# Pool projection of a decoder trunk, token-major: four seven-product units spread over three column groups, block moves split over two queues

## The chip, the cores and the metric

The kernel runs on one core of a Trainium2 chip. The metric is the device time of one execution in microseconds (us); for the kernel before it is 2051.21 us, the median of three runs (2050.52 to 2051.46). The core has five engines, each with its own instruction queue that runs in order: TensorE (PE), VectorE (DVE), ScalarE (ACT), GpSimd (POOL) and SyncE (SP). SP, POOL and ACT issue the transfers here.

## The reference

A decoder trunk of two layers on 256 tokens of 2048 channels, all in float32. Layer 0 mixes by causal pooling in four channel groups, layer 1 by dilated attention; each is followed by a gated convolutional feed-forward part, and each sublayer by a residual sum and a layer norm. What the change touches is the pooling mixer and the norm after it:

```python
def pool_mixer(h, w_in, w_grp, scale, w_out):
    p = (h @ w_in).reshape(B_, S, N_POOL_GROUPS, POOL_GROUP_DIM).astype(jnp.float32)
    ...
        outs.append((c - lag) / cnt - p[:, :, g])          # trailing mean over window 2, 4, 8, 16, less the token
    pooled = jnp.stack(outs, axis=2).astype(h.dtype)
    mixed = jnp.einsum('bsgc,gcd->bsgd', pooled, w_grp).reshape(B_, S, D) * scale
    return mixed @ w_out
...
        h = layer_norm(DEEPNORM_ALPHA * h + mix, ln1_g[i], ln1_b[i])
        ff = conv_ffn(h, ffn_w_up[i], ffn_conv_w[i], ffn_conv_b[i], ffn_w_down[i])
```

## The kernel before

**Precision and units.** Every float32 factor is split into a high part in a format that PE multiplies fast (float32r) and a low part with the rest; a product is three matmuls (high by high, high by low, low by high). The weights come in blocks of 512 x 512, one block a *unit*. For each unit SP loads the block (`raw`, L89), ACT copies the high part (`wh`, L99) and DVE subtracts it for the low part (`wl`, L100). `run_units` walks a list of units: at unit i it queues the load of unit i + 5 and the split of unit i + 3, then the matmuls of unit i, then whatever earlier steps put off to this point by `later(n, step)`, then the unit's own `post`. So the order of instructions in each engine's queue is fixed by the order of units and by these counts. Three `raw` blocks and four pairs of split weights can live at a time. PSUM holds four tiles of two banks each (`pair`, `two_banks`).

**Sevens.** A 2 x 2 blocked product normally takes eight block products. A unit given to `mk_seven` takes seven, by sums of blocks on both sides. It is two units in the list: "a" with 18 matmuls of 256 columns (three products) and "b" with 24 (four products). Its weights are prepared by `split_sums`: for "a" a copy on ACT (L119) and four subtractions on DVE (L120 to L124); for "b" two copies (L113) and two subtractions (L114). The sums on the activations' side come from `summed`, which makes `msums[g]` for a pool group g. Sevens use an extra pair of PSUM banks ("s"); when the last seven of a group is done, `early_post` folds those banks into a scratch tile, which POOL adds to the residual by an accumulating transfer (`onto`, L290) after the group's end, or DVE adds directly.

**The pool layer's end.** `pool_post` does the pooling, `grp_post` scales the group product, either through `summed` or by four scaled pairs (L628 on ACT, L629 on DVE). The output projection has tokens on the partitions (token-major, `group_tm`): four column groups c0 to c3 of 512 channels, each summing over four row blocks j, in the order written out in the last loop of the block. Before, c0 is all plain and comes among the last pool units; c1 and c2 have blocks 1 and 0 as sevens, c3 has 1 and 0 as sevens with block 2 last. The posts add the result to the residual `HT[c]` (L689, L691).

**Back to features.** The next part wants channels on the partitions. `begin` takes statistics of c0, finds a first mean and shifts all four groups by it (L711). `landed(c)` takes the statistics of a group and calls `to_features`: DVE transposes 32 x 32 blocks (L559), and `moves` sends 16 block transfers (L546) that put the blocks in place; for c0 to c2 by SP in three portions over three units, for c3 all at once over SP, POOL and ACT. Then `xp(c)` makes the scaled copy `XP[c]` (L427 on ACT, L428 on DVE) on which the feed-forward's first gate product runs before the norm is known. `ended` closes the statistics with c3, and `chain_tm` spreads them over the partitions: four copies on ACT (L450), then eight matmuls (`spread`, L455), put off by one unit, so that PE has the first gate unit ahead of it. `normed` and `norm_evac` then apply the norm.

The order of the units around the change, before: c0 block 3, c0 block 2, product of group 0, c0 block 1, c1 block 3, c0 block 0, and from there on c1 to c3 in their order; then the feed-forward's four gate units, the first ones that read `XP`.

Of the kernel before, what the change touches and what calls it, by code (L numbers as in the profile page):

```python
# [9 lines left out]
F32 = mybir.dt.float32  # L10
# [7 lines left out]
T = 256  # L18
# [14 lines left out]
def trunk(ctx: ExitStack, tc: tile.TileContext, x, pool_w_in, pool_w_grp, pool_scale, pool_w_out,  # L33
# [501 lines left out]

    def moves(fr, to, at_once=False):
        fr = fr.rearrange("p (k b j) -> p b k j", k=8, b=4)
        dst = []

        def part(i, n):  # L540
            if i == 0:
                dst.append(to().rearrange("p (k a j) -> p a k j", k=8, a=4))
            for ab in range(i, i + n):
                a, b = ab // 4, ab % 4
                by = (nc.sync, nc.gpsimd, nc.sync, nc.gpsimd, nc.scalar)[ab % 5] if at_once else nc.sync
                by.dma_start(dst[0][32 * b:32 * b + 32, a], fr[32 * a:32 * a + 32, b])  # L546

        if at_once:
            part(0, 16)
            return  # L550
        for k, (i, n) in enumerate(((0, 6), (6, 5), (11, 5))):
            later(k + 1, lambda i=i, n=n: part(i, n))

    def to_features(c, at_once=False):
        hb = hp.tile([P, 4, T], F32, name="hb", tag="h")
        hf = hb.rearrange("p m t -> p (m t)")
        V.transpose(hf.rearrange("p (m t c) -> p t m c", m=4, t=2), HT[c].rearrange("p t (m c) -> p t m c", m=4))  # L559

        def to():
            H[c] = hp.tile([P, 4, T], F32, name="h", tag="h")
            return H[c].rearrange("p m t -> p (m t)")

        moves(hf, to, at_once)

# [54 lines left out]
    def grp_post(g):  # L621
        def post(ps):
            mixed_q[g] = t = quad_tile("mixed")
            if g < 2:
                return summed(g, ps)
            for m in range(4):
                sc = vec[0][:, 64 + 4 * g + m:65 + 4 * g + m]
                A.activation(t[:, m, 0, :T], ps[m][:, :T], AF.Copy, scale=sc)  # L628
                V.scalar_tensor_tensor(t[:, m, 1, :T], ps[m][:, :T], sc, t[:, m, 0, :T].bitcast(F32),  # L629
                                       op0=OP.mult, op1=OP.subtract)  # L630
        return post
# [3 lines left out]
    def summed(g, ps):  # L635
# [8 lines left out]
        def two():  # L644
# [3 lines left out]
            V.tensor_tensor(d[3], a12, d[1], OP.subtract)  # L648
            hl = [pools["pool"].tile([P, 4, PADW + T], F32R, name="ms", tag=("pb", "sw")[g], bufs=2)[:, :, :T]
                  for i in range(2)]  # L650
            A.copy(hl[0], f)
# [33 lines left out]
    def out_post(c):  # L685
        def post(t, ps, half=None):
# [5 lines left out]
            if c == 3:  # L692
                ended(t)
            elif t == 1:
                if c == 0:
                    later(1, begin)
                later(2, lambda: landed(c))
                later(6, lambda: xp(c, 0, 0))
        return post

    def begin():
        ST["bn"] = bn = lnp.tile([P, 2, 5, 6], F32, name="bn", tag="bn")
        for t in range(2):
            mv = lnp.tile([P, 6], F32, name="mv", tag="mv", bufs=2)
            V.bn_stats(bn[:, t, 0, :], HT[0][:, t, :])
            V.bn_aggr(mv[:, 0:2], bn[:, t, 0:1])
            V.tensor_scalar(mv[:, 2:3], mv[:, 0:1], -1.0, None, op0=OP.mult)
            V.tensor_scalar(bn[:, t, 0, 1::3], bn[:, t, 0, 1::3], mv[:, 0:1], None, op0=OP.subtract)
            for c in range(4):
                y = HT[c][:, t, :]  # L710
                A.activation(y, y, AF.Identity, scale=1.0 if c == 0 else ALPHA, bias=mv[:, 2:3])  # L711

    def landed(c):
        if c > 0:
            for t in range(2):
                V.bn_stats(ST["bn"][:, t, c, :], HT[c][:, t, :])
        to_features(c)

    ends = []

    def ended(t):
# [5 lines left out]
        if t == 1:  # L727
            to_features(3, True)
        V.reciprocal(mv[:, 3:4], mv[:, 2:3])
# [6 lines left out]
    mark = len(units)  # L736
    for c, js in enumerate(((3, 2, 1, 0), (3, 1, 2, 0), (3, 1, 2, 0), (3, 1, 0, 2))):
        sv = {i: (lambda j=j: msums[j]) for i, j in enumerate(js) if c > 0 and j < 2}
        group_tm(pool_w_out[0], [(512 * j, 512) for j in js], 512 * c, 512, [lambda j=j: mixed_q[j] for j in js],
                 out_post(c), seven=sv, early=early_post(c, c < 3))  # L740
    outs = units[mark:]
    del units[mark:]
    units.extend(outs[:2])
    add_grp(0)
    units.extend([outs[2], outs[4], outs[3]] + outs[5:])
    marks.append(len(units))
# [540 lines left out]
    with tc.tile_pool(name="pool", bufs=1) as pp:  # L1287
        pools["pool"] = pp
        pools["pb"] = [pp.tile([P, 4, PADW + T], F32, name=f"pb{i}", tag="pb", bufs=2) for i in range(2)]
        for b in pools["pb"]:  # L1290
            V.memset(b[:, :, :PADW], 0.0)
        vrow, crow = [], []
        for l in range(2):
            n = 80 if l == 0 else 64
# [5 lines left out]
            vrow.append((r, n))  # L1300
            cr = pp.tile([2 * NF, 4, P], F32, name=f"crow{l}")
            nc.gpsimd.dma_start(cr[:, 0:3, :], ffn_conv_w[l].rearrange("j (k p) -> k j p", p=P))
# [87 lines left out]
```

## Time and profile before

| | |
|---|---|
| time, median of 3 runs | 2051.21 us |
| profiled execution | 2050.99 us, span 2049.2 us |
| PE busy | 2012.0 us (98%) |
| DVE busy | 1759.0 us (86%) |
| ACT busy | 1283.3 us (63%) |
| POOL busy | 100.2 us (5%) |
| granted TensorE clock, mean | 0.993 |
| weights and inputs read | 380.01 MB, 186 GB/s over the span |

The span is the time from the first to the last instruction. PE is busy in nearly all of it; matmuls are pipelined and their ends are modelled, so a busy PE need not be at its peak. The granted clock is the share of its full speed that PE was allowed. In a table of waits the idle time of an engine is put down to what came last; a chain of waits runs back from the last instruction. "x3" behind a line is a count, and a name such as `wl` stands for all buffers of that name.

### The profile page before, as it was taken

The numbers are of one execution on the slowest core, as the hardware profiler recorded it, in microseconds if no ns is written. First come the engines' busy times: TensorE is split into PE (matmuls) and PEld (weight loads), VectorE is DVE, ScalarE is ACT, GpSimd is POOL, SyncE is SP. The second block draws the span as 40 slices with busy tenths as digits, with TensorE's granted clock in tenths as the row PEclk, the third lists the DMA queues.
The fourth block names the chain that finished last, engine by engine and source line by source line (L and its number), as shares of the span: only waits on it lengthen the run. The fifth ranks groups of instructions, "written<-read, shape, count | busy, mean of one in ns | idle before, by whom it ended". The sixth has DMA issues, their size and how long they took to land.

```text
span 2049.2 us, 31450 instructions
## 1 busy us (share of the span) xinstructions
PE 2012.0 (98%) x12679; PEld 1811.1 (88%) x12679; DVE 1759.0 (86%) x1856; ACT 1283.3 (63%) x1567; POOL 100.2 (5%) x163
## 2 busy tenths in 40 slices
PE   9998599999999999999999999999999999999999
PEld 8887598899989989889898988998899989999987
DVE  6878787899899989879897868887799899989898
ACT  5454487766677667655654434568767676667673
POOL 2000100000000000000010111000000000000000
PEclk9999899999999999999999999999999999999999
DMA  8555667666756666886466666547666657676665
GB/s 246 205 174 148 178 208 206 165 221 199 226 177 216 208 227 183 237 249 201 165 166 220 202 182 198 189 161 223 190 198 219 216 168 227 198 230 197 202 213 181
DMA packets 287841, 410.91 MB, mean 201 GB/s; under 512 B 90366, under 2 KB 101524, under 8 KB 287440
## 3 DMA queue, kind: packets, MB, share of 16 engines
q1 hardware_dynamic: 274448, 390.74, 58.8%
q0 software_dynamic: 12000, 17.42, 5.6%
q8 instruction: 99, 1.62, 0.3%
q10 hardware_dynamic: 1248, 0.75, 0.1%
q14 instruction: 46, 0.38, 0.1%
HBM read 380.01 MB, written 2.10 MB: 186 GB/s over the span
## 4 chain that ended last, share of the span: by engine, by line
PE 88%; DVE 6%; DMA 3%; ACT 2%; issue 1%; SPq 1%; ACTq 0%; DVEq 0%
PE acc L180 39%; PE acc L181 20%; PE s L249 3%; PE s L247 3%; PE s L248 3%; PE t L249 2%; PE t L248 2%; PE t L247 2%; PE t L258 2%; PE t L259 2%; PE t L260 2%; PE acc L184 2%; PE acc L185 2%; PE acc L183 2%; DVE wl L100 2%
## 5 line engine op out<-in xcount | busy, mean ns | idle before, releaser
L180 PE MATMUL acc<-xc,wh 128*128 128x512 f32 x3264 | 1151.6, 396 | 0.0
L181 PE MATMUL acc<-xc,wl 128*128 128x256 f32 x3264 | 915.9, 281 | 0.9 <-DVE wl L100 0.9
L100 DVE TENSOR_TENSOR wl<-raw,wh 128x2048 fp32r<-128x2048 f32 (+2 forms) x298 | 641.6, 2160 | 162.2 <-ACT wh L99 157.6
L180 PEld LDWEIGHTS acc<-xc,wh 128*128 128x128 f32 x3264 | 616.0, 189 | 142.8 <-issue 0.3
L99 ACT CAST wh<-raw 128x2048 fp32r<-128x2048 f32 (+2 forms) x298 | 535.9, 1804 | 156.7 <-PE acc L180 53.9
L181 PEld LDWEIGHTS acc<-xc,wl 128*128 128x128 f32 x3264 | 615.2, 188 | 1.3 <-DVE wl L100 1.2
L113 ACT CAST wh<-raw 128x1024 fp32r<-128x1024 f32 x156 | 162.9, 1053 | 219.5 <-DVE raw L122 195.6
L114 DVE TENSOR_TENSOR wl<-raw,wh 128x1024 fp32r<-128x1024 f32 x156 | 186.1, 1222 | 16.0 <-ACT wh L113 16.0
L121 DVE TENSOR_TENSOR wl<-raw,wh 128x1536 fp32r<-128x1536 f32 x78 | 136.8, 1754 | 7.0 <-ACT wh L119 5.7
L119 ACT CAST wh<-raw 128x1536 fp32r<-128x1536 f32 x78 | 115.3, 1478 | 41.1 <-PE acc L180 24.5
L290 POOL DMA_DIRECT2D ht<-w x52 | 44.8, 1009 | 1440.0 <-DVE ht L977 582.7
L249 PE MATMUL t<-wh,g 128*128 128x256 f32 x376 | 105.6, 281 | 0.0
L248 PE MATMUL t<-wl,g 128*128 128x256 f32 x376 | 105.5, 280 | 0.0
L247 PE MATMUL t<-wh,g 128*128 128x256 f32 x376 | 105.5, 280 | 0.0
L785 ACT ACTIVATE c<-u,cv 128x256 f32<-128x256 f32 x172 | 89.5, 593 | 24.1 <-DVE f L847 16.4
L124 DVE TENSOR_TENSOR raw<-raw 128x1024 f32<-128x1024 f32 x78 | 95.6, 1225 | 2.7
L249 PE MATMUL s<-wh,xs 128*128 128x256 f32 x344 | 96.0, 279 | 0.0
L247 PE MATMUL s<-wh,xs 128*128 128x256 f32 x344 | 96.0, 279 | 0.0
L248 PE MATMUL s<-wl,xs 128*128 128x256 f32 x344 | 95.9, 279 | 0.0
L790 ACT ACTIVATE a<-u,cv 128x256 f32<-128x256 f32 x172 | 73.5, 500 | 11.9 <-DVE g L857 11.9
L776 ACT COPY u<-acc 128x512 f32<-128x512 f32 x84 | 46.7, 573 | 42.9 <-PE acc L181 42.8
L790 ACT ACTIVATE u<-u,cv 128x256 f32<-128x256 f32 x172 | 73.5, 501 | 0.0
(386 smaller groups left out, 3450.8 us busy)
## 6 DMA issues: line engine op xcount, KB each, us to landing
raw<-in_ffn_w_up_dram SPq DMA_DIRECT2D x160, 1024.0 KB, 5.1
raw<-in_ffn_w_down_dram SPq DMA_DIRECT2D x80, 1024.0 KB, 5.4
raw<-in_pool_w_out_dram SPq DMA_DIRECT2D x16, 1024.0 KB, 5.5
raw<-in_shared_w_k_dram SPq DMA_DIRECT2D x16, 1024.0 KB, 5.2
raw<-in_attn_w_q_dram SPq DMA_DIRECT2D x16, 1024.0 KB, 5.0
raw<-in_shared_w_v_dram SPq DMA_DIRECT2D x16, 1024.0 KB, 5.3
raw<-in_attn_w_o_dram SPq DMA_DIRECT2D x16, 1024.0 KB, 5.2
ht<-w POOLq DMA_DIRECT2D x54, 256.0 KB, 5.2
```

The lines of the kernel that those rows point to most:

```text
L99: A.copy(wh[i][:, s], r[:, s])
L100: V.tensor_tensor(wl[i][:, s], r[:, s], wh[i][:, s].bitcast(F32), OP.subtract)
L113: A.copy(h[:, :, n], r[:, :, n])
L114: V.tensor_tensor(l[:, :, n], r[:, :, n], h[:, :, n].bitcast(F32), OP.subtract)
L119: A.copy(hs, rs)
L121: V.tensor_tensor(ls, rs, hs.bitcast(F32), OP.subtract)
L180: PE.matmul(ps[m].ap, h[:, k, c], q[:, k, :, :T], start=st, stop=False)
L181: PE.matmul(ps[m][:, :T], l[:, k, c], q[:, k, 0, :T], start=False, stop=sp)
L247: PE.matmul(to, xh, h[:, k, n], start=opens and kk == 0, stop=False)
L248: PE.matmul(to, xh, l[:, k, n], start=False, stop=False)
L249: PE.matmul(to, xl, h[:, k, n], start=False, stop=ends and kk == 1)
L790: A.activation(to[:, m, :], u[:, m, i:i + T], AF.Copy, scale=cv[:, i, j:j + 1])
```

## The change

1. *Sevens.* All four column groups take the blocks in the order 3, 2, 1, 0. c0 has blocks 2 and 1 as sevens, c1 and c2 block 1, c3 none: four in place of six. Pool groups 1 and 2 make sums now, group 0 goes by the scaled pairs. c0's sums too are added by POOL.
2. *Order of units.* c0 block 3, both halves of c0's block 2, product of group 0, both halves of c0's block 1, c1 block 3, c0 block 0, and then the rest in order.
3. *Block moves.* For c0 to c2 POOL issues moves 0 to 7 and SP moves 8 to 11 at once, and SP the last four one unit later. For c3 the sixteen are dealt out anew: six to SP, seven to POOL, three to ACT.
4. *Scaled copies and shift.* `begin` comes two units after c0's end in place of one, c0's `landed` three in place of two, and `xp` 7, 5 and 5 units after the group's end in place of 6. The shift of c0 and c1 stays in `begin`, that of c2 and c3 comes two and three units later.
5. *Buffers.* The sums of group 2 lie in a block buffer of the `h` kind and in one that the convolution's parameter rows used earlier.

```diff
@@ -533,7 +533,7 @@
         return hp.tile([P, 4, T], F32, name="ht", tag="h").rearrange("p a t -> p (a t)").rearrange(
             "p (t c) -> p t c", t=2)
 
-    def moves(fr, to, at_once=False):
+    def moves(fr, to, by=None):
         fr = fr.rearrange("p (k b j) -> p b k j", k=8, b=4)
         dst = []
 
@@ -542,18 +542,18 @@
                 dst.append(to().rearrange("p (k a j) -> p a k j", k=8, a=4))
             for ab in range(i, i + n):
                 a, b = ab // 4, ab % 4
-                by = (nc.sync, nc.gpsimd, nc.sync, nc.gpsimd, nc.scalar)[ab % 5] if at_once else nc.sync
-                by.dma_start(dst[0][32 * b:32 * b + 32, a], fr[32 * a:32 * a + 32, b])
-
-        if at_once:
-            part(0, 16)
+                (by[ab] if by else nc.sync).dma_start(dst[0][32 * b:32 * b + 32, a], fr[32 * a:32 * a + 32, b])
+
+        if by:
+            part(0, 12)
+            later(0 if by[12] is nc.gpsimd else 1, lambda: part(12, 4))
             return
         for k, (i, n) in enumerate(((0, 6), (6, 5), (11, 5))):
             later(k + 1, lambda i=i, n=n: part(i, n))
 
 
 
-    def to_features(c, at_once=False):
+    def to_features(c, by=None):
         hb = hp.tile([P, 4, T], F32, name="hb", tag="h")
         hf = hb.rearrange("p m t -> p (m t)")
         V.transpose(hf.rearrange("p (m t c) -> p t m c", m=4, t=2), HT[c].rearrange("p t (m c) -> p t m c", m=4))
@@ -562,7 +562,7 @@
             H[c] = hp.tile([P, 4, T], F32, name="h", tag="h")
             return H[c].rearrange("p m t -> p (m t)")
 
-        moves(hf, to, at_once)
+        moves(hf, to, by)
 
 
     def early_post(c, by_dma):
@@ -621,7 +621,7 @@
     def grp_post(g):
         def post(ps):
             mixed_q[g] = t = quad_tile("mixed")
-            if g < 2:
+            if g in (1, 2):
                 return summed(g, ps)
             for m in range(4):
                 sc = vec[0][:, 64 + 4 * g + m:65 + 4 * g + m]
@@ -646,8 +646,10 @@
             V.tensor_tensor(d[1], d[0], a11, OP.subtract)
             V.tensor_tensor(d[2], a21, a11, OP.subtract)
             V.tensor_tensor(d[3], a12, d[1], OP.subtract)
-            hl = [pools["pool"].tile([P, 4, PADW + T], F32R, name="ms", tag=("pb", "sw")[g], bufs=2)[:, :, :T]
-                  for i in range(2)]
+            if g == 1:
+                hl = [pools["pool"].tile([P, 4, PADW + T], F32R, name="ms", tag="sw", bufs=2)[:, :, :T] for i in range(2)]
+            else:
+                hl = [hp.tile([P, 4, T], F32R, name="ms", tag="h"), pools["pool"].tile([P, 4, T], F32R, name="ms", tag="ms")]
             A.copy(hl[0], f)
             V.tensor_tensor(hl[1], f, hl[0].bitcast(F32), OP.subtract)
             msums[g] = [[z[:, i].rearrange("p (k t) -> p k t", k=2) for z in hl] for i in range(4)]
@@ -693,28 +695,35 @@
                 ended(t)
             elif t == 1:
                 if c == 0:
-                    later(1, begin)
-                later(2, lambda: landed(c))
-                later(6, lambda: xp(c, 0, 0))
+                    later(2, begin)
+                later(3 if c == 0 else 2, lambda: landed(c))
+                later((7, 5, 5)[c], lambda: xp(c, 0, 0))
         return post
 
     def begin():
         ST["bn"] = bn = lnp.tile([P, 2, 5, 6], F32, name="bn", tag="bn")
+        mvs = []
         for t in range(2):
             mv = lnp.tile([P, 6], F32, name="mv", tag="mv", bufs=2)
             V.bn_stats(bn[:, t, 0, :], HT[0][:, t, :])
             V.bn_aggr(mv[:, 0:2], bn[:, t, 0:1])
             V.tensor_scalar(mv[:, 2:3], mv[:, 0:1], -1.0, None, op0=OP.mult)
             V.tensor_scalar(bn[:, t, 0, 1::3], bn[:, t, 0, 1::3], mv[:, 0:1], None, op0=OP.subtract)
-            for c in range(4):
+            mvs.append(mv)
+
+        def less(c):
+            for t in range(2):
                 y = HT[c][:, t, :]
-                A.activation(y, y, AF.Identity, scale=1.0 if c == 0 else ALPHA, bias=mv[:, 2:3])
+                A.activation(y, y, AF.Identity, scale=1.0 if c == 0 else ALPHA, bias=mvs[t][:, 2:3])
+
+        for c in range(4):
+            later((0, 0, 2, 3)[c], lambda c=c: less(c))
 
     def landed(c):
         if c > 0:
             for t in range(2):
                 V.bn_stats(ST["bn"][:, t, c, :], HT[c][:, t, :])
-        to_features(c)
+        to_features(c, 8 * [nc.gpsimd] + 8 * [nc.sync])
 
     ends = []
 
@@ -725,7 +734,7 @@
         V.bn_aggr(mv[:, 0:2], bn[:, t, :4])
         A.activation(mv[:, 2:3], mv[:, 1:2], AF.Sqrt, bias=epst)
         if t == 1:
-            to_features(3, True)
+            to_features(3, (3 * [nc.sync, nc.gpsimd, nc.scalar, nc.gpsimd] + [nc.gpsimd, nc.sync, nc.sync, nc.sync]))
         V.reciprocal(mv[:, 3:4], mv[:, 2:3])
         V.tensor_tensor(mv[:, 4:5], mv[:, 0:1], mv[:, 3:4], OP.mult)
         ends.append(mv)
@@ -734,15 +743,15 @@
             later(2, lambda: xp(3, 0, 0))
 
     mark = len(units)
-    for c, js in enumerate(((3, 2, 1, 0), (3, 1, 2, 0), (3, 1, 2, 0), (3, 1, 0, 2))):
-        sv = {i: (lambda j=j: msums[j]) for i, j in enumerate(js) if c > 0 and j < 2}
+    for c, js in enumerate(((3, 2, 1, 0), (3, 2, 1, 0), (3, 2, 1, 0), (3, 2, 1, 0))):
+        sv = {i: (lambda j=j: msums[j]) for i, j in enumerate(js) if j in ((1, 2), (1,), (1,), ())[c]}
         group_tm(pool_w_out[0], [(512 * j, 512) for j in js], 512 * c, 512, [lambda j=j: mixed_q[j] for j in js],
-                 out_post(c), seven=sv, early=early_post(c, c < 3))
+                 out_post(c), seven=sv, early=early_post(c, True))
     outs = units[mark:]
     del units[mark:]
-    units.extend(outs[:2])
+    units.extend(outs[:3])
     add_grp(0)
-    units.extend([outs[2], outs[4], outs[3]] + outs[5:])
+    units.extend(outs[3:5] + [outs[6], outs[5]] + outs[7:])
     marks.append(len(units))
 
 
@@ -1286,10 +1295,11 @@
         run_units(3)
     with tc.tile_pool(name="pool", bufs=1) as pp:
         pools["pool"] = pp
-        pools["pb"] = [pp.tile([P, 4, PADW + T], F32, name=f"pb{i}", tag="pb", bufs=2) for i in range(2)]
+        pools["pb"] = [pp.tile([P, 4, PADW + T], F32, name=f"pb{i}") for i in range(2)]
         for b in pools["pb"]:
             V.memset(b[:, :, :PADW], 0.0)
         vrow, crow = [], []
+        crows = pp.tile([P, 2, 4, P], F32, name="crow", tag="ms")
         for l in range(2):
             n = 80 if l == 0 else 64
             r = pp.tile([80, P], F32, name=f"vrow{l}")
@@ -1298,7 +1308,7 @@
             if l == 0:
                 nc.gpsimd.dma_start(r[64:80], pool_scale[0].rearrange("(k p) -> k p", p=P))
             vrow.append((r, n))
-            cr = pp.tile([2 * NF, 4, P], F32, name=f"crow{l}")
+            cr = crows[:2 * NF, l]
             nc.gpsimd.dma_start(cr[:, 0:3, :], ffn_conv_w[l].rearrange("j (k p) -> k j p", p=P))
             nc.gpsimd.dma_start(cr[:, 3, :], ffn_conv_b[l].rearrange("(k p) -> k p", p=P))
             crow.append(cr)
```

## The prediction, made before the changed kernel was timed

> **What bounds the kernel now.** First the page: TensorE (PE) is busy nearly all the time, so a gain can only come from where it is not.
>
> ```profile
> span 2049.2 us, 31450 instructions
> PE 2012.0 (98%) x12679; PEld 1811.1 (88%) x12679; DVE 1759.0 (86%) x1856; ACT 1283.3 (63%) x1567; POOL 100.2 (5%) x163
> PE   9998599999999999999999999999999999999999
> PEclk9999899999999999999999999999999999999999
> ```
>
> Slice 5 (205 to 256 us) is half idle, and only there does the granted clock dip. The waits of PE name the causes, nearly all in the pool layer's output projection and the layer norm behind it:
>
> ```profile
> PE spread L455 <- ACT st L450: 12.9, 1, 12.9
> PE s L248 <- DVE wl L121: 4.8, 2, 3.4
> PE s L247 <- ACT wh L119: 3.8, 2, 3.3
> PE t L259 <- DVE wl L100: 3.7, 3, 1.3
> PE s L248 <- DVE wl L114: 2.7, 2, 1.8
> ```
>
> That is 27.9 us: 12.9 before the spread of the norm's statistics, 15.0 before weights whose low part VectorE (DVE) or whose high part ScalarE (ACT) had not finished. The chain that ended last (start, length, what) says what the 12.9 is made of: DVE reaches the last residual late, at 248.86, and from there it is 5.5 us through the transpose, three moves that ACT issues and the copies of the statistics to the spread, which runs at half clock (1.1 at full):
>
> ```profile
> 248.86 0.61 DVE ht L691
> 250.48 1.10 DVE hb L559
> 253.88 0.41 ACT st L450
> 254.33 2.23 PE spread L455 x8
> ```
>
> The windows give the place (columns: length, then PE, PEld, DVE, ACT, POOL busy; granted clock; DMA share):
>
> ```profile
> 122.75:156.35 33.60, 33.60 (x171) 28.25 (x170) 25.36 (x24) 17.68 (x19) 0.00 (x0) 1.00 0.42 141
> 166.90:188.00 21.10, 17.81 (x115) 15.61 (x114) 17.15 (x16) 10.60 (x11) 1.79 (x2) 1.00 0.57 139
> 188.00:209.00 21.00, 17.23 (x87) 14.18 (x86) 18.23 (x20) 10.57 (x12) 0.00 (x0) 0.92 0.53 134
> 209.00:235.50 26.50, 18.52 (x110) 16.79 (x109) 21.14 (x23) 11.32 (x13) 1.70 (x2) 0.87 0.74 210
> 235.50:256.20 20.70, 7.79 (x57) 7.50 (x56) 11.15 (x21) 7.90 (x14) 3.56 (x6) 0.77 0.63 160
> ```
>
> Column group c0 and the last pool group's projection run without a wait, and DVE has 8 us free there. In c1 to c3 PE starves and the clock falls as well; one such wait, from PE's timeline:
>
> ```profile
> 200.18 0.39 PE L248 MATMUL s<-wl,ms 128*128 128x256 f32 x1 [1.78 <-DVE wl L114]
> ```
>
> PE's timeline fixes the units and my anchor, the first L180 matmul of the feed-forward, at 275.37:
>
> ```profile
> 139.60 0.40 PE L258 MATMUL t<-wh,mixed 128*128 128x512 f32 x1
> 156.35 0.28 PE L247 MATMUL s<-wh,mixed 128*128 128x256 f32 x1
> 161.33 0.39 PE L258 MATMUL t<-wh,mixed 128*128 128x512 f32 x1
> 269.65 0.29 PE L183 MATMUL acc<-xp,wh 128*128 128x258 f32 x1
> 275.37 0.40 PE L180 MATMUL acc<-xc,wh 128*128 128x512 f32 x1
> ```
>
> Three plain units take 16.75, so 5.58 each; a seven 4.98; a gate unit 5.72. Work from 156.35 to the anchor: 5 plain, 6 sevens, 4 gate units and 1.1 for the spread = 81.8 of 119.0 us. **Lost: 37.2**, of it 27.9 waits and 9.3 half clock, 0.33 us of clock per us of wait.
>
> **The change, part by part.** *Sevens.* Their price is on DVE:
>
> ```profile
> L100 DVE TENSOR_TENSOR wl<-raw,wh 128x2048 fp32r<-128x2048 f32 x17 | 38.6, 2286 | 8.9 <-ACT wh L99 8.9
> L114 DVE TENSOR_TENSOR wl<-raw,wh 128x1024 fp32r<-128x1024 f32 x12 | 14.3, 1221 | 4.8 <-ACT wh L113 4.8
> L121 DVE TENSOR_TENSOR wl<-raw,wh 128x1536 fp32r<-128x1536 f32 x6 | 10.5, 1756 | 0.4 <-ACT wh L119 0.4
> L124 DVE TENSOR_TENSOR raw<-raw 128x1024 f32<-128x1024 f32 x6 | 7.4, 1226 | 0.2
> L120 DVE TENSOR_TENSOR raw<-raw 128x512 f32<-128x512 f32 x6 | 4.1, 687 | 0.0
> L559 DVE STREAM_TRANSPOSE hb<-ht 128x1024 f32<-128x1024 f32 x4 | 4.9, 1222 | 0.0
> L629 DVE SCALAR_TENSOR_TENSOR mixed<-acc,vec,mixed 128x256 fp32r<-128x256 f32 x4 | 1.8, 482 | 1.1 <-ACT mixed L628 1.1
> ```
>
> A seven's split is 0.7 twice (L120 and its twin), 1.8, 1.2 and 1.2 twice: 6.7 us, against 2.3 plain. It saves PE 0.60. So c1 now asks of DVE 13.4 + 4.6 for splits and 7.0 for sums (1.5), residual and statistics (1.3 each), transpose (1.2) and scaled copy (1.7): 25 us against 21.1 of PE. Afterwards c1 and c2 have one seven each: 6.7 + 6.9 + 7 = 20.6 against 21.7; c3 has none, 9.2 + 4 against 22.3; c0's two fall where DVE had 8 us free, of which they take 8.8. PE pays 2 x 0.60 = **+1.2**. Total DVE work falls by some 9 us, and c0 to c2 fit.
>
> *Pooled sums.* Those of group 2 replace those of group 0; same instructions, but three units ahead of c0 and so before 122.75, where none of PE's waits in the table lies. Group 0 gets the scaled pair L628/L629 instead, in turn with ACT. Their buffers (one block buffer, one shared with the convolution rows) are free by then: 0.
>
> *Scaled copies later.* Now eight in a row hold ACT and then DVE:
>
> ```profile
> 163.13 5.02 ACT L711 ACTIVATE ht<-ht,mv 128x512 f32<-128x512 f32 x8 [5.11 <-DVE mv L707]
> 169.12 2.36 DVE L114 TENSOR_TENSOR wl<-raw,wh 128x1024 fp32r<-128x1024 f32 x2 [4.75 <-ACT wh L113]
> ```
>
> Four at once (2.5), then two and two in later units: half of DVE's 4.75 idle goes.
>
> *Block moves.* Today all 16 of c0 to c2 are on SP, between weight loads:
>
> ```profile
> 172.72 4.01 SPq L546 DMA_DIRECT2D h<-hb  x6
> 176.82 5.68 DMA raw<-in_pool_w_out_dram
> 182.58 1.91 ACT L99 CAST wh<-raw 128x2048 fp32r<-128x2048 f32 x1 [2.16 <-DMA raw<-in_pool_w_out_dram]
> ```
>
> A load queued behind six moves came 2.2 late for ACT. Four ahead of a load instead of six saves 2 x 0.65 of SP per load, but SP still waits there for the transpose. POOL's share:
>
> ```profile
> 252.25 3.56 POOL L546 DMA_DIRECT2D h<-hb  x6 [31.74 <-issue]
> ht<-w POOLq DMA_DIRECT2D x4, 256.0 KB, 4.7
> DMA to landing us min/median/max: 3.3/5.2/10.1
> ```
>
> 0.59 a move, so eight take 4.8, beside SP's, and land well before the scaled copies that need them, which now come one unit later for c0 and one earlier for c1 and c2. If that cover went (each landing at 10.1 in place of 4.7) ACT would stand 4 us at c1's copies, and PE lose some 2. c3's sixteen are dealt out in another order, with ACT's three as before. POOL has three accumulations (c0's is new) and 31 moves in 100 us; the wait to note is the new one: the centring statistics of c0 are queued on DVE and ACT behind c0's accumulation.
>
> **What is late next.** I lay each engine's queue in program order from 97 us on, with the durations above. Three things set it: the split of a unit is queued three units ahead of its matmuls; its buffers come free when PE has finished the unit four before; and each post, sum and statistic stands in DVE's and ACT's queues between the splits where the unit loop puts it. In c0 the splits come out just ahead of PE (the second half of c0's second seven at 141.2, the very time at which PE comes to it). The last pooling is over today when DVE turns to this split:
>
> ```profile
> 121.28 2.28 DVE L100 TENSOR_TENSOR wl<-raw,wh 128x2048 fp32r<-128x2048 f32 x1
> ```
>
> Three waits of PE remain.
>
> (1) c1's first unit. DVE leaves the last pooling at 122.6, 1.3 later than today, since the first half of a seven (4.3) now stands ahead of it in place of a plain split; then a seven's second half 2.4, two low parts 2.4, a plain split 2.3, group 1's sums 2.9, a seven 6.7, c1's split 2.3, = 19.0, and 2.4 waiting for ACT: 144.0, just when PE comes (122.75 + 5.58 + 2 x 4.98 + 5.7 = 144.0). But all four pairs of PSUM banks are held (two by c0, two by group 0), and one comes free only after DVE, ACT, DVE in turn (3 x 0.48): PE waits about **1.5**.
>
> (2) From 144.0 DVE goes on with group 0's scaled pairs (2.9, in turn with ACT), 1.4 of waiting for ACT's next copy, two plain splits (4.6), the sums of c0's sevens (1.5), c1's seven (6.7) and c0's residual (1.3): 162.3. The accumulation has landed at 167 to 168 (4.7 from issue); statistics to 169.3; four scaled copies to 171.8; the next split, ACT then DVE, 4.2, to 176.0; transpose 177.2; four moves on SP to 179.8; the load behind them to 186; its split to 190.2. PE wants it at 189: **1.2**.
>
> (3) The end. From 190.2 on: c1's statistics and transpose 2.5, four moves on SP 2.6 (195.3), the load behind them 5.7 (201), its split 4.2, c1's scaled copy 1.7, c2's residual 1.3 (208.1), its accumulation 5.6 with the issue of both (213.7), statistics and transpose 2.5, two splits 4.6: 220.8. PE ends c3 at 217.9. From DVE's last residual to the spread the chain shown above takes 5.5 us, three moves issued by ACT in it, and the change leaves that so. First half of c3 2.1, so the second starts at 222.9 and the spread at 228.4; PE's first gate unit ends at 223.6: **4.8**, where today it is 12.9.
>
> Waits 7.5, clock at 0.33 of that 2.5, work 1.2: 11.2 in place of 37.2. **Gain 26.0.** The profiled execution took 2050.99 (span 2049.2 and 1.8 around it): 2025.0. The median shown, 2051.21, is 0.2 above it. What lies behind the anchor I leave alone: c2's scaled copy now stands behind the norm's statistics instead of ahead of them (1.7 more for ACT and DVE there), so DVE comes into the norm some 4 us closer to PE than today, but by the same walk each of its pieces is still ready within a microsecond of its need. Bounds of that: 0, and 2 for PE's three further units there.
>
> Two rules of the Trainium skill bear on this. The clock: with no wait over 1.8 in the stretch from 188 to 209 the granted clock was still 0.92. "TensorE: Matmul & The Clock Gate", Part 1, puts the half clock behind an idle window of 3.4 us; by it only the 4.8 would cost, 1.7, and the gain would be 26.8; the row contradicts it. The queues: "DMA: Bandwidth & Descriptors", in "Issuing engines are not separate DMA queues", says that spreading over issuers saves only issue time, since all share 16 engines; by it the moves gain nothing past SP's 1.3 per load, which is all I count.
>
> **Rivals.**
> *All waits go*, gain 35 to 36 (37.2 less 1.2), 2015: if loads come earlier than I lay them, (1) to (3) shrink together. For it: DVE's free time in c3. Against: SP still waits for each transpose.
> *The sevens left still starve PE and the end stays late*: 15.0 of waits over six sevens is 2.5 each, 5 for c1's and c2's, and 10 to 13 at the spread; with clock 20 to 24, work 1.2: gain 12 to 16, 2037. For it: DVE is 95% full from c0 to c2. A variant that does not do what it says: moves on POOL land at 10.1 as the slowest transfer of that queue did, and scaled copies stand in ACT's queue until then.
> *No change*: the spread stays at 12.9 and each of the three groups loses 5.
> *Slower*: the half clock. By the clock column it held for 3.4, 6.9 and 9.5 us of the last three windows shown (twice the shortfall times the length), after waits as short as 1.8. If many small waits in place of few long ones hold it through the stretch, 116 us of work lose up to 58; slower from about 60 us at half clock. Against: c0 runs at 1.00 without a wait.
>
> **How the numbers follow.** Forecast 0.60 (gain 19 to 33), all gone 0.17, starved 0.16 (gain 5 to 18), no change 0.03, slower 0.04. 0.2% (4 us) is about what a measurement of this kernel tells from no change. Faster 0.93, same 0.03, slower 0.04. Low end 2016 (gain 35), high end 2037 (14); the ends are the bounds of the first two rivals.
>
> **What would show it.** In the profile after: no L121 wait of PE in c3; s waits under 1 us each; the spread's wait near 5 and after an ACT wait for moves; a wait of one or two us at c1's first t matmul, released by DVE L629; a load late behind L546 on SP; the first L180 of the feed-forward near 249; granted clock above 0.9 throughout. Wrong if the spread still waits 10 or more, if ACT's copy L427 waits for POOL's moves, or if PE waits in c0, whose slack I have spent to the last microsecond.

## The result and the profile after

The changed kernel takes 2035.07 us (median of 4 runs, 2033.52 to 2038.28), the kernel before 2050.86 beside it (4 runs): a ratio of 0.9927, 95% interval 0.991 to 0.9945, 15.8 us faster. The forecast was 2025.0 with a range of 2016 to 2037: the sign and the range hold, the size is 10 us short. The profiled execution took 2036.04, 14.95 less than that of before.

The page of the changed kernel, its first lines, the slices of PE and of the granted clock:

```profile
span 2034.3 us, 31405 instructions
PE 2007.6 (99%) x12643; PEld 1805.9 (89%) x12643; DVE 1748.4 (86%) x1844; ACT 1279.9 (63%) x1563; POOL 116.4 (6%) x190
PE   9999799999999999999999999999999999999999
PEclk9999899999999999999999999999999999999999
```

PE is busy 4.4 us less and DVE 10.6. The same slice (now 203 to 254 us) is the one in which PE idles and the clock dips, but seven tenths busy where it was five. PE's waits from 118 to 262 us (total, times, longest) and the rows that fix the stretch, its timeline:

```profile
PE spread L455 <- ACT st L450: 13.2, 1, 13.2
PE t L259 <- DVE wl L100: 3.6, 2, 1.8
PE s L248 <- DVE wl L114: 0.3, 1, 0.3
```

```profile
122.11 0.40 PE L258 MATMUL t<-wh,mixed 128*128 128x512 f32 x1
...
189.86 0.50 PE L259 MATMUL t<-wl,mixed 128*128 128x512 f32 x1 [1.82 <-DVE wl L100]
...
197.44 0.50 PE L259 MATMUL t<-wl,mixed 128*128 128x512 f32 x1 [1.73 <-DVE wl L100]
...
259.34 0.40 PE L180 MATMUL acc<-xc,wh 128*128 128x512 f32 x1
```

Waits for weights went from 15.0 to 3.9. The wait before the spread did not move: 12.9 before, 13.2 now. From c0's first matmul to the anchor it is 137.23 us, where it was 275.37 - 122.75 = 152.62: 15.4 gained in the stretch. (c0 itself starts 0.64 earlier, since PE stood still 3.8 us ahead of it where it was 4.4, in waits for its first inputs and weights; the same kernel run again starts c0 at 122.54. Of the 16.0 at the anchor 1.1 is lost behind it; the prediction allowed 0 to 2 there.)

The windows (length, then PE, PEld, DVE, ACT, POOL busy; granted clock; DMA share) of c0, of the two late loads, of the spread, and behind it:

```profile
121.40:155.00 33.60, 33.60 (x215) 30.21 (x214) 28.42 (x30) 18.02 (x20) 0.00 (x0) 1.00 0.54 184
188.00:209.00 21.00, 17.45 (x75) 13.82 (x75) 14.92 (x17) 10.17 (x15) 4.70 (x8) 1.00 0.90 254
225.00:240.60 15.60, 2.45 (x14) 2.16 (x12) 6.36 (x12) 3.15 (x8) 6.11 (x11) 0.66 0.80 187
240.60:260.00 19.40, 19.40 (x150) 19.31 (x150) 18.55 (x19) 16.75 (x26) 0.00 (x0) 0.92 0.68 214
```

c0 carries two sevens and PE does not wait there. From 188 to 209 the clock is whole (0.92 before), but the share of the DMA engines is 0.90 (0.53 before). At 225 to 240.6 PE works 2.45 of 15.6 us; the granted clock falls to 0.66 there and is still 0.92 in the last window. What holds the spread is read on DVE and on ACT:

```profile
190.86 0.69 DVE L725 BATCH_NORM_STATS2 bn<-ht 128x6 f32<-128x512 f32 x1 [1.05 <-DMA ht<-w]
192.92 0.69 DVE L725 BATCH_NORM_STATS2 bn<-ht 128x6 f32<-128x512 f32 x1 [1.36 <-DMA ht<-w]
...
218.21 0.69 DVE L725 BATCH_NORM_STATS2 bn<-ht 128x6 f32<-128x512 f32 x1 [2.79 <-DMA ht<-w]
220.26 0.69 DVE L725 BATCH_NORM_STATS2 bn<-ht 128x6 f32<-128x512 f32 x1 [1.36 <-DMA ht<-w]
...
228.74 0.68 DVE L693 TENSOR_TENSOR ht<-ht,t 128x512 f32<-128x512 f32 x1
...
234.35 1.25 DVE L559 STREAM_TRANSPOSE hb<-ht 128x1024 f32<-128x1024 f32 x1 [3.91 <-DMA h<-hb]
```

```profile
235.63 2.51 ACTq L545 DMA_DIRECT2D h<-hb  x3
238.25 1.28 ACT L450 ACTIVATE st<-onesd,mv 128x128 f32<-128x128 f32 x4 [7.48 <-DMA h<-hb]
```

Then the spread, in PE's timeline, 9.96 us behind the last residual half:

```profile
238.70 2.23 PE L455 MATMUL spread<-ident,st 128*128 128x128 f32 x8 [13.15 <-ACT st L450]
```

Two kinds of delay stand in this chain. The statistics of c1 (first two lines) and of c2 (next two) wait for the accumulations of their groups, 2.4 and 4.2 us. That of c2 was issued at 211.00:

```profile
211.00 1.79 POOL L290 DMA_DIRECT2D ht<-w  x2 [10.99 <-DVE ht L693]
```

so the second half is read 9.3 us after the issue of both, where 5.6 was counted. That of c1, issued at 183.34, is read 9.6 us later, and there no wait was counted. And c3's transpose waits 3.91 for block moves: for transfers that *read* the block buffer it wants to write, c2's last ones, as a kernel below with another buffer bears out. The transfers of 165 to 245 us (count, size, median us to landing):

```profile
raw<-in_pool_w_out_dram SPq DMA_DIRECT2D x5, 1024.0 KB, 6.9
ht<-w POOLq DMA_DIRECT2D x4, 256.0 KB, 8.1
```

The accumulations land in 8.1 us where before it was 4.7.

### The profile page after: what moved, and what is told of

Read it like the earlier page. It is cut to its first block, busy times and chain, and to the rows that moved or that the text cites. A ratio compares the mean times of both kernels' runs of the same rounds, so it can differ in the third digit from the quotient of the medians.

```text
span 2034.3 us, 31405 instructions
## 1 busy us (share of the span) xinstructions
PE 2007.6 (99%) x12643; PEld 1805.9 (89%) x12643; DVE 1748.4 (86%) x1844; ACT 1279.9 (63%) x1563; POOL 116.4 (6%) x190
## 3 DMA queue, kind: packets, MB, share of 16 engines
q8 instruction: 99, 1.62, 0.3%
## 4 chain that ended last, share of the span: by engine, by line
PE 49%; DVE 8%; ACT 2%; issue 1%; DMA 1%; DVEq 0%; ACTq 0%
PE acc L180 23%; PE acc L181 12%; DVE wl L100 2%; PE s L249 2%; PE s L247 2%; PE s L248 2%; PE t L248 1%; PE t L249 1%; PE t L247 1%; ACT wh L99 1%; PE acc L184 1%; PE acc L183 1%; PE acc L185 1%; DVE wl L121 1%; PE t L258 1%
## 5 line engine op out<-in xcount | busy, mean ns | idle before, releaser
L114 DVE TENSOR_TENSOR wl<-raw,wh 128x1024 fp32r<-128x1024 f32 x152 | 181.3, 1221 | 11.3 <-ACT wh L113 11.3
```

The lines of the kernel that those rows point to most:

```text
L114: V.tensor_tensor(l[:, :, n], r[:, :, n], h[:, :, n].bitcast(F32), OP.subtract)
```

## The experiments

Each kernel was timed beside the kernel before on one chip. "Stretch" is from c0's first t matmul to the anchor, in the profiled execution. The three after the changed kernel do one part of the change alone; the rest start from the changed kernel.

| kernel | median us (range) | ratio (95%) | stretch us | spread waits us |
|---|---|---|---|---|
| changed | 2035.07 (2033.52 to 2038.28) | 0.9927 (0.991 to 0.9945) | 137.23 | 13.2 |
| sevens alone | 2042.32 (2041.39 to 2043.24) | 0.9961 (0.9947 to 0.9975) | 146.00 | 7.4 |
| moves alone | 2051.65 (2050.2 to 2054.42) | 1.0007 (0.9998 to 1.0017) | 153.83 | 15.6 |
| shift alone | 2045.31 (2043.64 to 2046.81) | 0.9974 (0.9964 to 0.9983) | 147.82 | 13.2 |
| own buffer | 2029.53 (2028.56 to 2029.88) | 0.9899 (0.9885 to 0.9914) | 131.76 | 8.8 |
| + c2's sums by DVE | 2026.22 (2025.2 to 2026.65) | 0.9883 (0.9866 to 0.9899) | 128.33 | 3.7 |
| + c1's and c2's by DVE | 2024.91 (2023.81 to 2025.42) | 0.9875 (0.986 to 0.989) | 127.63 | 5.0 |
| own buffer, old moves | 2037.43 (2034.49 to 2038.45) | 0.9935 (0.992 to 0.9949) | 139.17 | 5.8 |
| own buffer, old shift | 2034.09 (2032.46 to 2036.26) | 0.9921 (0.9906 to 0.9936) | 138.10 | 9.9 |
| c1, c2 by DVE, no ACT moves | 2024.43 (2023.04 to 2026.49) | 0.9873 (0.9859 to 0.9888) | 125.67 | 2.3 |
| c1, c2 by DVE, 16 moves on POOL | 2026.76 (2026.5 to 2027.05) | 0.9884 (0.9869 to 0.9899) | 128.78 | 5.7 |
| both of these | 2028.4 (2026.03 to 2029.91) | 0.9891 (0.9876 to 0.9906) | 130.83 | 1.6 |
| changed, again | 2035.52 (2031.86 to 2036.81) | 0.9921 (0.9904 to 0.9937) | 138.33 | 11.8 |

**The three parts, each alone.** *Sevens alone*: the new order, sevens and sums, with moves, shift and scaled copies as before; c3's transpose has a block buffer of its own here, without which the old three portions of c2's moves would still be due when it comes.

```diff
-    def to_features(c, by=None):
-        hb = hp.tile([P, 4, T], F32, name="hb", tag="h")
+    def to_features(c, at_once=False):
+        hb = (pools["pool"].tile([P, 4, T], F32, name="hb", tag="ms") if at_once
+              else hp.tile([P, 4, T], F32, name="hb", tag="h"))
...                                # moves(), begin() and the counts 1, 2, 6 as before
```

> The change's sevens, unit order and buffers alone: block moves as before (SP, three portions; c3's over three queues in the old order), shift and scaled copies at the old counts. With the old portions c3's transpose would stand ahead of c2's last portion and wait for it for ever, so c3's transposed blocks lie in a buffer of their own. Theory A (what starved TensorE was VectorE's load from the sevens): most of the 15.0 us of waits for weights goes, to 3 to 6 us; 10 to 18 us faster than before, spread's wait 9 to 14. Theory B (SP's block moves ahead of weight loads were the cause): waits for weights stay at 10 or more, less than 6 us faster.

8.2 us faster, between the two. PE's waits:

```profile
PE spread L455 <- ACT st L450: 7.4, 1, 7.4
PE t L259 <- DVE wl L100: 4.2, 2, 2.6
PE t L258 <- ACT wh L99: 4.2, 2, 2.2
PE acc L183 <- ACT xp L430: 4.0, 1, 4.0
```

No seven waits any more, so the split over three groups does what it says. But the plain units now wait 8.4 for their high and low parts, and c2's scaled copy comes 4.0 late for the third gate unit: a queue that was just as late before now shows on PE. ACT waits for loads that stand behind SP's moves, and its scaled copies for the moves themselves:

```profile
ACT xp L427 <- DMA h<-hb: 12.3, 2, 6.4
ACT wh L99 <- DMA raw<-in_pool_w_out_dram: 9.6, 2, 7.5
```

In the changed kernel ACT has no wait for moves at its scaled copies, in that of before 14.6 us:

```profile
ACT xp L427 <- DMA h<-hb: 14.6, 3, 5.2
```

*Moves alone*: the kernel before, with the new `moves` and its lists.

```diff
-        to_features(c)
+        to_features(c, 8 * [nc.gpsimd] + 8 * [nc.sync])
...
-            to_features(3, True)
+            to_features(3, (3 * [nc.sync, nc.gpsimd, nc.scalar, nc.gpsimd] + [nc.gpsimd, nc.sync, nc.sync, nc.sync]))
```

> The kernel before with the change's block moves alone (POOL and SP at once for c0 to c2, c3's dealt anew). Theory A: waits for weights 12 to 15 us, time within 3 us of before. Theory B: waits for weights under 8, 8 us faster or more; weight loads land in 6 us or less.

No difference (1.0007, interval 0.9998 to 1.0017). The sevens are still starved, 8.1 us in place of 11.3, and the spread waits 2.7 longer:

```profile
PE spread L455 <- ACT st L450: 15.6, 1, 15.6
PE s L248 <- DVE wl L121: 5.5, 2, 4.1
...
```

The loads of the projection did not land sooner either (7.4 us, median, 165 to 245 us; 6.8 before). That DVE, full in c1 and c2, is why the moves gain nothing here fits, but this run does not show it.

*Shift alone*: the kernel before with the new `begin` and new counts; with the old portions of moves the scaled copies need 7, 6 and 6 units.

```diff
-                    later(1, begin)
-                later(2, lambda: landed(c))
-                later(6, lambda: xp(c, 0, 0))
+                    later(2, begin)
+                later(3 if c == 0 else 2, lambda: landed(c))
+                later((7, 6, 6)[c], lambda: xp(c, 0, 0))
```

> The kernel before with the split shift alone (c0 and c1 at once, c2 and c3 two and three units later, statistics one unit later; scaled copies at 7, 6 and 6 units, since with the old three portions of moves 5 would be too early). Theory A: only the two waits right behind the shift (0.9 and 1.2 us) go, time within 3 us of before. Rival: the shift's hold on ScalarE delays all that follows, 6 us faster or more.

5.2 us faster, between the two. PE's waits in the stretch are 23.7 us in place of 27.9, and the spread's stays:

```profile
PE spread L455 <- ACT st L450: 13.2, 1, 13.2
...
PE s L248 <- DVE wl L121: 3.4, 1, 3.4
...
```

Alone the parts give 8.2, nothing and 5.2 (against the 2050.5 of their runs), together 13.4 with a buffer for c3 that the changed kernel, at 15.8, does not have.

**The block buffer.** Only c3's block buffer is changed: it takes one that the sums of group 2 have left by then.

```diff
-        hb = hp.tile([P, 4, T], F32, name="hb", tag="h")
+        hb = (pools["pool"].tile([P, 4, T], F32, name="hb", tag="ms") if by and c == 3
+              else hp.tile([P, 4, T], F32, name="hb", tag="h"))
```

> The changed kernel with one edit: c3's transposed blocks lie in a buffer of their own, not in one that c2's moves must leave first. Theory C (the 3.9 us wait of that transpose for c2's last moves is on the path to the spread): transpose follows the statistics at once, the spread's wait falls from 13.2 to 9 to 9.5, 4 to 5.5 us faster than the changed kernel (2029.5 to 2031). Rival D (ScalarE's queue, held by loads and moves, is as late): spread's wait 12 to 13, no more than 1.5 us faster.

5.5 us faster than the changed kernel. On DVE, the last residual and the transpose:

```profile
227.84 0.68 DVE L694 TENSOR_TENSOR ht<-ht,t 128x512 f32<-128x512 f32 x1
...
229.46 1.19 DVE L560 STREAM_TRANSPOSE hb<-ht 128x1024 f32<-128x1024 f32 x1
```

1.62 us from one to the other, as before the change (248.86 to 250.48), in place of 5.61: that wait was the buffer. The changed kernel, run once more, has the wait again, and 11.8 at the spread, just under what was expected.

> The changed kernel unedited, on the same chip as these three: 2033 to 2038, spread's wait 12 to 14, a wait of c3's transpose of 3 to 5 us for c2's moves. If that wait were an accident of one profile it would be gone here, and the time nearer 2031.

```profile
236.44 1.25 DVE L559 STREAM_TRANSPOSE hb<-ht 128x1024 f32<-128x1024 f32 x1 [3.75 <-DMA h<-hb]
```

**The accumulations.** With the own buffer, c2's seven sums are added by DVE directly instead of by POOL's transfer; then c1's as well (`c < 1`).

```diff
-                 out_post(c), seven=sv, early=early_post(c, True))
+                 out_post(c), seven=sv, early=early_post(c, c < 2))
```

> The changed kernel with c3's own buffer (e4, 2029.5) and c2's folded sums added to its residual by VectorE at once, not by POOL's accumulating transfer. Theory E (that transfer, 6 to 9 us beside weight loads, delays c2's transpose and the loads beside it): c2's statistics no longer wait for it (3.7 us in e4), loads beside it land in 6 us, the spread's wait falls from 8.8 to 4 to 6, 3 to 5 us faster than e4. Rival F (the loads alone time the splits ahead of the last residual, and VectorE pays 1.4 more): spread's wait 7.5 to 9, within 1.5 us of e4.

> As e5, with c1's folded sums added by VectorE as well; only c0's go by POOL. Theory E: the loads of c2's last and c3's first unit land 2 us earlier, the waits of 1.7 and 0.9 there go, 1 to 3 us faster than e5. Rival F: VectorE's 1.4 more in a group that has a seven costs TensorE what it saves; within 1.5 us of e5.

The first gains another 3.3 us. Its last residual half, on DVE, comes 3.8 earlier, and the spread waits 3.7 in place of 8.8. The loads beside it land no sooner, though, in 7.0 us (median) where theory E had 6 and the kernel with the own buffer 6.9:

```profile
224.00 0.68 DVE L694 TENSOR_TENSOR ht<-ht,t 128x512 f32<-128x512 f32 x1
```

The second gains 1.3 more, which both its expectations admit; what c1's accumulation alone costs is not settled. Its last residual half comes 100.60 us after c0's first matmul (222.47 - 121.87), where the prediction had 100.15 (222.9 - 122.75) and the changed kernel 106.63. Its waits and the anchor, from PE's table of waits, PE's timeline and DVE's:

```profile
PE spread L455 <- ACT st L450: 5.0, 1, 5.0
PE t L259 <- DVE wl L100: 1.4, 1, 1.4
```

```profile
249.50 0.40 PE L180 MATMUL acc<-xc,wh 128*128 128x512 f32 x1
```

```profile
222.47 0.68 DVE L694 TENSOR_TENSOR ht<-ht,t 128x512 f32<-128x512 f32 x1
```

These are close to the forecast's own numbers (4.8 at the spread, 1.2 for the late load, anchor 249, 2025.0). So the walk through the queues comes near a kernel without these waits, in part by errors that cancel: c2's residual ends 1.6 later than laid, and the 5.6 laid for its accumulation are 4.5 here, for the two splits that DVE runs between the residual and the statistics.

**What moves and shift are worth beside the sevens.** The own-buffer kernel, once with the old moves (three portions on SP, one to three units later, scaled copies 7, 6 and 6, c3's dealt as before), once with the old shift and counts (1, 2, 6).

```diff
-        to_features(c, 8 * [nc.gpsimd] + 8 * [nc.sync])
+        to_features(c)             # by SP in portions of 6, 5, 5
...
-                later((7, 5, 5)[c], lambda: xp(c, 0, 0))
+                later((7, 6, 6)[c], lambda: xp(c, 0, 0))
```

> The changed sevens, order, shift and counts with c3's own buffer, but block moves as before (SP alone, three portions; scaled copies of c1 and c2 at 6 units, which the three portions need). Against e4 this is the moves' share on top of the rest. Theory G (once the sevens no longer starve TensorE, SP's 16 moves ahead of weight loads do): 4 to 9 us slower than e4 (2033.5 to 2038.5), waits of t matmuls 4 to 9 us. Rival (moves worth nothing, as alone): within 2 us of e4.

> The changed sevens, order and moves with c3's own buffer, but shift of all four groups at once and the old counts (statistics after 1 unit, landed 2, scaled copies 6). Against e4 this is the shift's share on top of the rest. If it is worth what it was alone: 4 to 6 us slower than e4 (2033.5 to 2035.5), a wait of 2 to 4 us of TensorE right behind the shift. Rival (it gained alone only because VectorE was overfull with sevens): within 2 us of e4.

Without the new moves 7.9 us slower (4 to 9 expected); without the spread shift 4.6 slower (4 to 6). The old moves' waits of PE, then of ACT, and a row of DVE:

```profile
PE spread L455 <- ACT st L450: 5.8, 1, 5.8
PE t L259 <- DVE wl L100: 5.6, 1, 5.6
PE acc L183 <- ACT xp L430: 3.7, 1, 3.7
```

```profile
ACT xp L427 <- DMA h<-hb: 17.1, 3, 6.0
```

```profile
196.62 1.25 DVE L560 STREAM_TRANSPOSE hb<-ht 128x1024 f32<-128x1024 f32 x1 [4.42 <-DMA h<-hb]
```

PE's wait of 5.6 ends at 200.1, behind the split that DVE ran next, at 197.79, and the transpose of c1 ahead of it had waited 4.42 for a block buffer that c0's third portion, issued from 187.07 to 192.35, still read. So the old moves cost by landing late: ACT's scaled copies wait 17.1 for them (0.4 with the new ones), and the block buffers are held. The two waits behind the old shift, in PE's timeline:

```profile
172.94 0.49 PE L258 MATMUL t<-wh,mixed 128*128 128x512 f32 x1 [2.21 <-ACT wh L99]
...
175.26 0.50 PE L259 MATMUL t<-wl,mixed 128*128 128x512 f32 x1 [1.83 <-DVE wl L100]
```

So the new moves are worth nothing alone and 7.9 beside the new sevens. How much of the 7.9 is the second queue and how much that the moves no longer wait for later units is not separated: the edit puts both back.

**Past the forecast.** From the kernel with c1's and c2's sums by DVE: ACT's three moves are taken off (c3's by SP and POOL alone); or the moves of c0 to c2 all by POOL; or both.

```diff
-            to_features(3, (3 * [nc.sync, nc.gpsimd, nc.scalar, nc.gpsimd] + [nc.gpsimd, nc.sync, nc.sync, nc.sync]))
+            to_features(3, 8 * [nc.sync, nc.gpsimd])
```

```diff
-        to_features(c, 8 * [nc.gpsimd] + 8 * [nc.sync])
+        to_features(c, 16 * [nc.gpsimd])
```

> e6 (2024.9) with c3's sixteen moves dealt to SP and POOL in turn, none to ScalarE. Theory H (the three issues on ScalarE, 2.3 us, stand in the path to the spread): the copies of the statistics start 2.3 us earlier, the spread's wait falls from 5.0 to 2.5 to 3, and with it some of the half clock; 2 to 4 us faster than e6. Rival: the last moves then leave later and the scaled copy of c3 (XP of the fourth gate unit) comes late by as much; within 1 us of e6.

> e6 with all sixteen moves of c0 to c2 on POOL, none on SP. If SP's wait for the transposes is what makes the load behind them late (my second wait): the wait of 1.4 us at c2's last unit goes, 1.5 to 3 us faster than e6. Rival (the moves and loads share the transfer engines, whoever issues): load still 6.5 to 7 us, wait stays over 1 us, within 1 us of e6.

> e9 and e10 together. If the two are separate causes, their gains add: 3.5 to 6 us faster than e6. If both only move the same wait at the spread, no better than the better of the two.

Without ACT's moves the spread waits 2.3 in place of 5.0, but the median is the same within 0.5 us, as the rival expected (the profiled executions differ by 1.7). PE's waits from c0 on add up to 7.9, where they were 7.4, since a new one stands at the anchor; PE's waits from 215 to 250 us and ACT's scaled copy:

```profile
PE acc L180 <- DVE xc L308: 2.4, 1, 2.4
PE spread L455 <- ACT st L450: 2.3, 2, 1.8
```

```profile
237.10 1.71 ACT L427 ACTIVATE xp<-h,vec 128x256 fp32r<-128x256 f32 x4 [4.25 <-DMA h<-hb]
```

c3's scaled copy now waits 4.25 for c3's moves, three of which ACT had issued itself, and the norm's pieces behind it are late: the wait has moved. The edit does one thing more than it says: `moves` puts the last four off by a unit unless POOL issues the thirteenth, which SP does here, so two of them leave SP only at 231.40, behind a weight load. Whether the wait comes from that or from the missing queue is open. With all moves of c0 to c2 on POOL the loads of the projection land in 5.3 us (median, 165 to 245 us; 6.1 without), yet the kernel is 1.9 slower, which neither expectation had: the moves themselves end late, and ACT's scaled copy, c1's, stands for them.

```profile
207.70 1.71 ACT L427 ACTIVATE xp<-h,vec 128x256 fp32r<-128x256 f32 x4 [10.03 <-DMA h<-hb]
```

Both together are 3.5 slower than with neither, again outside what was expected; ACT waits for moves four times, 20.2 us in all.

```profile
ACT xp L427 <- DMA h<-hb: 20.2, 4, 11.9
```

The best version is the changed kernel with its own block buffer for c3 and c1's and c2's sums added by DVE, with or without ACT's moves: 2024.4 to 2024.9, some 10 us ahead of the changed kernel and 25 to 26 ahead of the one before.

## Why the prediction was right, and where its size failed

*Sevens: right.* All waits on a seven's weights but 0.34 us are gone, and c0 takes its two sevens without a wait, as the 8 us free there said. The sevens alone, with c3's own buffer, give 8.2.

*Shift and scaled copies: right in kind, too small.* The prediction gave them half of DVE's 4.75 us; alone they gave 5.2, put back they cost 4.6, with two units behind the old shift waiting 2.2 and 1.8.

*Block moves: counted by the wrong gain.* The prediction counted SP's issue time, 1.3 per load. Put back, the old moves cost 7.9, and they land late: scaled copies and transposes wait for them. The Trainium skill, "DMA: Bandwidth & Descriptors", section "Issuing engines are not separate DMA queues", says that spreading saves only issue time; the kernel with moves alone agrees (no gain). The 7.9 neither bears the rule out nor contradicts it, since the old portions are also issued units later. For the sum this did no harm: the walk laid each move where it comes.

*Step (1), the PSUM pair at c1's first unit, 1.5: not in the changed kernel's profile.* The pair came free as PE arrived. It does show, released by DVE's scaled pair, with 0.6 to 1.2 us in nine of the other kernels, the changed one run again among them. Predicted as a near tie, and a near tie it is.

*Step (2), the load behind SP's moves, 1.2: right, and short by one.* It measured 1.8 at 189.86. A second wait of 1.7, at 197.44, was not forecast: a load issued at 182.9 reached ACT only at 193.15. All waits but the spread's: 3.9, forecast 2.7, so 1.2 of the miss.

*Step (3), the end, 4.8: wrong, 13.15.* This is 8.4 of the 10.6 us by which the stretch's gain (15.4) stays under the forecast (26.0), and three of its terms failed. "c1's statistics and transpose 2.5" left out that they wait for c1's accumulation: 2.4 on DVE. With the load behind SP's four moves, which ACT could read 6.6 after them where 5.7 was counted, c2's residual came 3.5 late (counted from c0's start). "Its accumulation 5.6 with the issue of both" was mis-sized: it took 9.3. With 0.7 won behind the landing, the last residual half is 6.5 late. And "the chain takes 5.5, and the change leaves that so" failed: 9.96 us, 3.9 of it the block buffer. The prediction priced the buffers of the sums at 0 ("free by then") and did not look at the buffer of the block moves themselves: c2's moves were late with its accumulation, and c3's transpose found the last of them still reading. PE's own first gate unit came 2.6 later than forecast, which takes that much off the wait (6.5 + 4.5 - 2.6 = 8.4). The runs bear the last two out: an own buffer takes the spread's wait to 8.8, and c2's sums by DVE as well take it to 3.7. The first is read from the rows; with c1's sums by DVE too its statistics wait no more, and the kernel gains 1.3.

*Clock: the sum near, by luck.* 2.5 was forecast. The last 1.0 of the miss (10.6 less 8.4 and 1.2) would make it 3.5, but the clock column accounts for some 2.5: short by 0.34 of 15.6 us and 0.08 of 19.4 us in the last two windows, the half clock held for 13.7 us, and PE worked in 5.0 of them (1.9 from the spread to 240.60, 3.1 after), which costs half. Where the other 1.0 went stays open. The rate failed: at 0.33 per us the 17.0 us of waits would have cost 5.6. Most of them are one wait, and for most of the half clock PE stood still. The clock dips in this one spell (0.66 and 0.92, so not above 0.9 throughout), which agrees with the rule of the Trainium skill's "TensorE: Matmul & The Clock Gate", Part 1, that the half clock follows an idle window. But in the kernel with c2's sums by DVE the granted clock fell too, behind two waits of 1.0 and 1.8 and none longer; its window:

```profile
190.00:195.00 5.00, 4.08 (x13) 3.25 (x14) 4.02 (x5) 2.65 (x4) 0.64 (x1) 0.74 0.81 279
```

while the kernel without ACT's moves, with a longest wait of 2.4, kept 1.00 in the whole stretch. So waits of this size may or may not cost clock, and 0.33 per us is a mean that a single kernel need not follow.

*The rivals.* By its number, "the sevens left still starve PE and the end stays late" is the case that came: it gave a gain of 12 to 16, and 15.4 was measured in the stretch. Its second half was right (10 to 13 at the spread; 13.2), its first was not: what PE still waits for in c1 to c3 is loads, in plain units, and not the splits of sevens. Its variant, scaled copies that stand in ACT's queue for moves on POOL, came only where all sixteen were put there (10.0). "All waits go", "no change" and "slower by half clock" did not come. Of the three signs that would make the prediction wrong, one came, the spread's wait of 10 or more, so by its own sign its account of the end is wrong; PE does not wait in c0, and ACT's copies do not wait for moves. That the time lies in the range is in part luck: its upper end, 2037, is this rival's, and the time is 2 us inside it.

What stays open: why the accumulations are slow (8.1 for 4.7). The order of POOL's queue alone is not the cause: the sevens alone, with the old moves, show 8.4 and the own buffer with the old moves 6.4, though POOL issues no move of c0 to c2 there. In all kernels with the new sevens that still have them they take 6.4 to 8.9, with the old sevens 4.2 to 5.8 (5.8 with the new moves). Loads that stand beside them are one reading of that; no run varies the loads, or what DVE does meanwhile, alone.

## What to carry to other kernels

When work moves earlier, look at who still *reads* the buffers that it writes: a rotating buffer that used to be free becomes a wait that no count of instructions shows. An edit tested alone need not show its worth beside the others (the moves: 0 alone, 7.9 together). A landing time read in one profile need not hold in the next (4.7 became 8.1); where the change puts a transfer on the path to the end, take the slow end of the old rows for it, and ask at each statistic whether it must wait for one.

## What was not expected of the hardware

Accumulating transfers of 256 KB went from 4.7 to 8.1 us (median) in a kernel whose DMA share between 188 and 209 us is 0.90 where it was 0.53, while the projection's 1 MB loads went from 6.8 to 6.9: of the two only the small ones took longer. With c2's accumulation gone (sums by DVE) those loads landed in 7.0, with c1's gone too in 6.1. Where POOL issues sixteen moves in a row, its row shows a pause that earlier moves ended:

```profile
201.03 3.04 POOL L545 DMA_DIRECT2D h<-hb  x5 [1.31 <-DMA h<-hb]
```
